# Order of operand stores and result loads on the SyncE queue at the turn from the up projection to the down projection

## The chip, the cores and the metric

The kernel runs on one core of a Trainium2 chip. The metric is the device time of one execution in microseconds (us); the time of a version is the median of its runs.

## What is computed

One step of a one-layer hybrid encoder over 640 tokens (512 of a prompt and 8 x 16 of samples), all in float32: an input projection, two groups of attention heads, an output projection, and a SwiGLU feed-forward network with a residual and a final norm. The change touches the feed-forward network only. Of the reference this is:

```
def merge_and_ffn(x, oa, ob, norm_grp_a, norm_grp_b, w_out, norm_ffn, w_gate, w_up, w_down):
    o = jnp.concatenate([rmsnorm(oa, norm_grp_a), rmsnorm(ob, norm_grp_b)], axis=-1)
    x = x + o @ w_out
    h = rmsnorm(x, norm_ffn)
    return x + (jax.nn.silu(h @ w_gate) * (h @ w_up)) @ w_down
```

The model width is 2048, the feed-forward width 5632 (44 tiles of 128, taken as 22 pairs, numbered 0 to 21).

## The kernel before

Tensors lie with features on the 128 partitions and tokens along the row; the 640 tokens are two halves of 320. Every float32 product is made from three reduced-precision matmuls: an operand is split into a high part (ScalarE writes it, rounded) and a low part (VectorE subtracts the high part from the source), and `mm3` (lines 204 to 206) multiplies high by high, high by low and low by high.

The feed-forward products use a seven-product scheme for 2 x 2 blocks (`quartet`, from line 880 on). One quartet takes four blocks of weights, forms three sums of them on VectorE and two on GpSimd (lines 932 and 941), splits each of seven weight operands (lines 195 and 196), and yields seven products, in the order p1, p6, p7, p2, p5, p4, p3. The right-hand operands are seven prepared combinations of the activations, called `which` 0 to 6, each with its two split halves in one tile of 128 x 640.

**Gate and up.** For each of the 22 pairs there is one quartet for `w_gate` and one for `w_up` with eight tiles a block, so 24 matmuls a product. After a pair's up quartet its seven combinations are formed. They must be kept for the down projection and SBUF can't hold those of 22 pairs, so `store_part` writes one of them to DRAM after each product that follows: split, as two transfers of 128 x 320 to `act_d` (ScalarE writes the high part into a scratch tile `half`, line 992, of which there are two; VectorE the low part, line 994; stores at lines 995 and 996), or, for the pairs in `raw_pairs`, unsplit, as one transfer to `first_d`.

**Down.** There are 32 steps. Step t adds to two tiles of the result, q = t % 8 and q + 8, the contributions of the pairs that `active(t)` lists: a pair stays active for eight steps in turn, so five or six pairs are in SBUF at a time. Pairs 0 to 4 are active in step 0; their last steps in this first round are 0, 2, 3, 5 and 6. A step is one quartet with five or six tiles a block, 7 x 5 x 3 = 105 matmuls for five. In the first eight steps the two result tiles (the residual `x2_d`) are loaded when the step is emitted (lines 1081 and 1082).

**The turn.** During the last up quartet, after each product, `free(which)` (lines 963 to 979) frees the gate/up operands of that `which` and brings in those of the five pairs of step 0: the pairs in `raw_pairs` (1, 2, 3) are loaded unsplit from `first_d` by SyncE, two pairs a load, and split there: the high part on ScalarE (line 973), the low part on VectorE for the first of a load and on GpSimd for the second (line 974). Pairs 0 and 4 are loaded split from `act_d` by a DMA that GpSimd issues (`fetch`, line 958). When a pair is given up in steps 0 to 7, its tiles go back to the free list, and if it is in `raw_pairs`, its split form is first written to `act_d`, for use in a later round (line 1074). The operands of the pair that comes next are fetched by GpSimd into tiles from the free list.

**What sets the order.** The program emits instructions in the order of the Python code. A scheduler then orders each engine's queue; within the data dependences it may issue a transfer ahead of others that were emitted before it. SyncE issues nearly all loads and stores, one after the other, and one that waits holds up those behind it; GpSimd's queue, too, is in order and holds its elementwise work and the operand fetches. Functions named `keep_...` add ordering edges: `keep_turns` lets a buffer's users stay in order, and `keep_behind` (lines 153 to 169) keeps the ScalarE instructions recorded in `n.behind` behind the last instruction on that engine emitted before them. Tiles come from 62 buffers `S` of 128 x 640 and 12 buffers `W` of 128 x 1024; a buffer that is put back is the last to be taken again.

Of the kernel before, what the change touches and what calls it, by code (L numbers as in the profile page):

```python
# [13 lines left out]
P = 128  # L14
# [3 lines left out]
HT = 320  # L18
# [31 lines left out]
class Net:  # L50
# [104 lines left out]
    def keep_behind(self):  # L155

        info = mybir.DependencyInfo(mybir.DependencyClass.NoSync, mybir.DependencyReason.DATA)
        for k, block in enumerate(self.nc.cur_f.blocks):
            inside = [0] * (len(block.instructions) + 1)
            for a, b in self.behind:  # L160
                if k < len(a):
                    inside[a[k]:b[k]] = [1] * (b[k] - a[k])
            last = None
            for i, ins in enumerate(block.instructions):
                if ins.engine == mybir.EngineType.Activation:
                    if not inside[i]:
                        last = ins
                    elif last is not None:
                        self.tc.add_manual_dep(ins, last.name, info, reason="behind")

    def keep_held(self):

# [127 lines left out]
def build(nc, tc, io, pools):  # L300
    n = Net(nc, tc, io, pools)
# [15 lines left out]
    def dram(name, shape):  # L317
        return pools["dr"].tile(list(shape), F32, tag=name, name=name)
# [491 lines left out]
    own_b, acts_b = group_operands(ob_d, g_b, ssq, range(8))  # L810
    n.add("decode", decode_a(1))
    x2_d, act_d = dram("x2_d", (KT, P, TOK)), dram("act_d", (7, P, NPAIR, 2, HT))
    first_d = dram("first_d", (7, P, 3, HT))
    r_a, ssq_a = n.get("S"), n.get("S")
    for m in range(KT):
        ps = n.dense([(io["w_out_b"][m], 8)], acts_b)
# [141 lines left out]
        nc.gpsimd.dma_start(out=r(sh(t, 2, HT)), in_=r(act_d[which, :, j]))  # L958
        lefts[j][which] = t, hl

    raw_pairs = active(0)[1:4]

    def free(which):
        n.put("S", *(h[which][0] for h in hs))
# [100 lines left out]
    def step(t, part="all"):  # L1065
# [4 lines left out]
        def after(which):  # L1070
            gone = [j for j in now if j not in nxt]
            for j in gone:
                if j in raw_pairs and t < 8:
                    dma(out=act_d[which, :, j], in_=sh(lefts[j][which][0], 2, HT))
            n.put("S", *(lefts[j][which][0] for j in gone))
            waiting.append([(j, which) for j in nxt if j not in now])
            fetch_waiting(2)

        if t < 8:
            x, y = n.get("S"), n.get("S")  # L1080
            dma(out=x, in_=x2_d[q])
            dma(out=y, in_=x2_d[q + 8])
            sums.append((x, y, n.get("S") if q % 2 == 0 else sums[-1][2]))
        x, y, u = sums[q]
        c11, c21, c12, c22 = x[:, :HT], x[:, HT:], y[:, :HT], y[:, HT:]
# [3 lines left out]
        for name, bank in quartet(cnt, load, [lefts[j] for j in now], None, after, part):  # L1089
# [20 lines left out]
                add(c21, c21, bank)  # L1110
            elif name == "p3":
                add(c12, c12, bank)
            store_part()
            yield name

    def run(*args):
# [51 lines left out]
    at = n.emitted()  # L1168
# [99 lines left out]
```

## Time and profile before

| | us |
|---|---|
| median of 3 runs | 2648.95 |
| lowest and highest run | 2647.41, 2651.69 |
| the profiled execution's own time | 2648.2 |
| span of its profile | 2646.4 |

The profile is of one execution. Of its span PE (the matmul engine, TensorE) is busy 98%, VectorE (DVE) 75%, ScalarE (ACT) 40% and GpSimd (POOL) 25%. The page divides the span into 40 slices of 66 us; in all but a few of them PE is at 9 tenths or more. The chain of waits is made of PE for 72%, of VectorE for 5% and of DMA for 4%. The granted TensorE clock over the span is 0.994 of full speed.

### The profile page before, as it was taken

What the parts mean: (1) busy time and instruction counts of PE and PEld (TensorE: products, weight loads), DVE (VectorE), ACT (ScalarE), POOL (GpSimd) and SP (SyncE); (2) the same over time, 40 slices, a digit from 0 to 9 for tenths busy, and PEclk for the clock granted to TensorE, in tenths of its full rate; (3) what the DMA queues carried; (4) which work ended last, traced back from release to release, by engine and by line L of the source; (5) the groups of instructions that cost most, each with busy time, mean ns of one, the idle gap of its engine ahead of it and who ended that gap; (6) DMA issues with size and microseconds to landing.
All of it is one profiled execution on the core that took longest, in us unless ns stands there. A gap on an engine that the chain in (4) does not pass through costs nothing.

```text
span 2646.4 us, 45166 instructions
## 1 busy us (share of the span) xinstructions
PE 2584.1 (98%) x17565; PEld 2527.2 (95%) x17565; DVE 1978.9 (75%) x3071; ACT 1069.3 (40%) x1732; POOL 662.1 (25%) x577
## 2 busy tenths in 40 slices
PE   8999999999999999999999999999999799999997
PEld 8999998999899999999999999999999799999996
DVE  5665566655866888768888888888887677777797
ACT  5443344444633553333443433433444333333343
POOL 0000000000201203333333233233234432333353
PEclk9999999999999999999999999999999899999998
DMA  5322232434655433333433433433436975665655
GB/s 170 105 70 83 87 101 92 129 116 133 216 186 183 156 127 123 115 106 123 142 130 125 140 130 125 144 132 120 150 128 214 372 201 155 170 184 169 185 155 178
DMA packets 178678, 388.47 MB, mean 147 GB/s; under 512 B 21856, under 2 KB 70496, under 8 KB 178464
## 3 DMA queue, kind: packets, MB, share of 16 engines
q1 hardware_dynamic: 153120, 329.21, 38.5%
q0 software_dynamic: 24192, 55.06, 7.3%
q8 instruction: 138, 2.26, 0.4%
q10 hardware_dynamic: 1152, 1.31, 0.1%
q14 instruction: 76, 0.62, 0.1%
HBM read 301.90 MB, written 82.87 MB: 145 GB/s over the span
## 4 chain that ended last, share of the span: by engine, by line
PE 72%; DVE 5%; DMA 4%; ACT 1%; issue 1%; POOL 0%; SPq 0%; DVEq 0%; ACTq 0%
PE dn L204 15%; PE dn L206 15%; PE dn L205 14%; PE at L204 9%; PE at L206 9%; PE at L205 9%; DVE W L196 2%; DMA W<-w_down 1%; PE at L321 1%; DVE S L951 1%; DMA act_d<-half 1%; DMA S<-cka 0%; DMA S<-first_d 0%; ACT W L195 0%; PE at L402 0%
## 5 line engine op out<-in xcount | busy, mean ns | idle before, releaser
L204 PE MATMUL dn<-S,W 128*128 128x320 f32 x3694 | 1158.3, 314 | 5.0 <-ACT W L195 4.4
L206 PE MATMUL dn<-S,W 128*128 128x320 f32 x3694 | 1145.1, 310 | 12.2 <-DVE W L196 12.2
L205 PE MATMUL dn<-S,W 128*128 128x320 f32 x3694 | 1143.8, 310 | 1.1 <-DVE S L200 0.8
L195 ACT ACTIVATE W<-W 128x1024 fp32r<-128x1024 f32 (+2 forms) x632 | 608.2, 963 | 977.5 <-PE dn L205 542.5
L196 DVE TENSOR_TENSOR W<-W,W 128x1024 fp32r<-128x1024 f32 (+2 forms) x632 | 738.4, 1169 | 91.8 <-ACT W L195 88.3
L204 PEld LDWEIGHTS dn<-S,W 128*128 128x128 f32 x3694 | 695.0, 188 | 17.5 <-ACT W L195 6.1
L206 PEld LDWEIGHTS dn<-S,W 128*128 128x128 f32 x3694 | 694.4, 188 | 17.1 <-DVE W L196 15.9
L205 PEld LDWEIGHTS dn<-S,W 128*128 128x128 f32 x3694 | 694.8, 188 | 3.6 <-DVE S L200 1.0
L204 PE MATMUL at<-S,W 128*128 128x320 f32 x1594 | 494.5, 310 | 7.5 <-ACT W L195 7.5
L206 PE MATMUL at<-S,W 128*128 128x320 f32 x1594 | 495.0, 311 | 4.3 <-DVE W L196 4.3
L205 PE MATMUL at<-S,W 128*128 128x320 f32 x1594 | 493.9, 310 | 0.0
L932 POOL TENSOR_TENSOR W<-W,W 128x1024 f32<-128x1024 f32 (+2 forms) x75 | 159.4, 2126 | 641.9 <-DVE W L196 404.8
L204 PEld LDWEIGHTS at<-S,W 128*128 128x128 f32 x1594 | 300.6, 189 | 8.3 <-ACT W L195 8.3
L206 PEld LDWEIGHTS at<-S,W 128*128 128x128 f32 x1594 | 300.4, 188 | 6.5 <-DVE W L196 6.5
L205 PEld LDWEIGHTS at<-S,W 128*128 128x128 f32 x1594 | 300.5, 189 | 0.0
L951 DVE TENSOR_TENSOR S<-S,dn 128x320 f32<-128x320 f32 x358 | 163.7, 480 | 71.1 <-PE dn L206 71.0
L941 POOL TENSOR_TENSOR W<-W,W 128x1024 f32<-128x1024 f32 (+2 forms) x75 | 162.9, 2173 | 115.0 <-DVE W L196 105.1
L927 DVE TENSOR_TENSOR W<-W,W 128x1024 f32<-128x1024 f32 (+2 forms) x76 | 122.4, 1610 | 70.1 <-DMA W<-w_down 36.5
L951 DVE TENSOR_TENSOR S<-S,at 128x320 f32<-128x320 f32 x262 | 123.2, 480 | 51.4 <-PE at L206 50.5
L958 POOL DMA_DIRECT2D S<-act_d x168 | 91.7, 547 | 185.6 <-PE dn L206 94.5
L929 DVE TENSOR_TENSOR W<-W,W 128x1024 f32<-128x1024 f32 (+2 forms) x76 | 83.4, 1097 | 63.0 <-DMA W<-w_up 34.2
L994 DVE TENSOR_TENSOR S<-S,half 128x320 fp32r<-128x320 f32 x133 | 115.1, 886 | 13.5 <-ACT half L992 11.6
(153 smaller groups left out, 2125.8 us busy)
## 6 DMA issues: line engine op xcount, KB each, us to landing
S<-act_d POOLq DMA_DIRECT2D x168, 320.0 KB, 3.9
W<-w_gate SPq DMA_DIRECT2D x88, 512.0 KB
W<-w_up SPq DMA_DIRECT2D x88, 512.0 KB
W<-w_in SPq DMA_DIRECT2D x66, 512.0 KB
W<-w_down SPq DMA_DIRECT2D x64, 384.0 KB
W<-w_down SPq DMA_DIRECT2D x68, 320.0 KB
act_d<-half SPq DMA_DIRECT2D x133, 160.0 KB
act_d<-S SPq DMA_DIRECT2D x133, 160.0 KB
```

The lines of the kernel that those rows point to most:

```text
L195: self.nc.scalar.activation(hi, src, AF.Identity)
L196: self.nc.vector.tensor_tensor(lo, src, f(hi), ALU.subtract)
L204: mm(out, a[0], b[0], start=first, stop=False)
L205: mm(out, a[0], b[1], start=False, stop=False)
L206: mm(out, a[1], b[0], start=False, stop=last)
L927: nc.vector.tensor_tensor(b12[:, w], b12[:, w], b22[:, w], sub)
L929: nc.vector.tensor_tensor(s6[:, w], b11[:, w], b12[:, w], sub)
L932: eng.tensor_tensor(b11[:, w], b22[:, w], s6[:, w], sub)
L941: eng.tensor_tensor(b21[:, w], b21[:, w], s6[:, w], sub)
L951: add = lambda o, a, b: nc.vector.tensor_tensor(o, a, b, ALU.add)
L958: nc.gpsimd.dma_start(out=r(sh(t, 2, HT)), in_=r(act_d[which, :, j]))
L994: nc.vector.tensor_tensor(r(src), src, hi, ALU.subtract)
```

## The change

Three edits, on the functions `keep_behind`, `free`, `step` and the table `raw_pairs`:

1. `keep_behind` is extended from ScalarE to SyncE, and the SyncE transfers of two places are recorded in `n.behind`: the stores of given-up operand tiles (line 1074 before, 1076 after) and the loads of the two result tiles (1081 and 1082 before, 1085 and 1086 after). On SyncE each of them is issued behind the last transfer not so recorded that was emitted before it.
2. `raw_pairs` grows from the pairs 1, 2, 3 to 1, 2, 3, 4. Pair 4 is written unsplit to `first_d` in the gate/up part, split at the turn, and its split form is stored to `act_d` when it is given up at the end of step 6.
3. The seven combinations of the last pair (21) are stored from step 2 on, not from step 0 on. (One part is stored directly behind the last up quartet, as before.)

```
@@ keep_behind
-            last = None
-            for i, ins in enumerate(block.instructions):
-                if ins.engine == mybir.EngineType.Activation:
-                    if not inside[i]:
-                        last = ins
-                    elif last is not None:
-                        self.tc.add_manual_dep(ins, last.name, info, reason="behind")
+            for engine in (mybir.EngineType.Activation, mybir.EngineType.SP):
+                last = None
+                for i, ins in enumerate(block.instructions):
+                    if ins.engine == engine:
+                        if not inside[i]:
+                            last = ins
+                        elif last is not None:
+                            self.tc.add_manual_dep(ins, last.name, info, reason="behind")
@@ build
-    first_d = dram("first_d", (7, P, 3, HT))
+    first_d = dram("first_d", (7, P, 4, HT))
-    raw_pairs = active(0)[1:4]
+    raw_pairs = active(0)[1:]
@@ step
                 if j in raw_pairs and t < 8:
+                    at = n.emitted()
                     dma(out=act_d[which, :, j], in_=sh(lefts[j][which][0], 2, HT))
+                    n.behind.append((at, n.emitted()))
...
             x, y = n.get("S"), n.get("S")
+            at = n.emitted()
             dma(out=x, in_=x2_d[q])
             dma(out=y, in_=x2_d[q + 8])
+            n.behind.append((at, n.emitted()))
...
-            store_part()
+            if t > 1:
+                store_part()
             yield name
```

How the queues stand before and after, at three places. In the rows, an operand `S_3183_21528` is a tile in an S buffer (the numbers only tell tiles apart), `W_...` a weight tile, `half_...` a scratch tile; a row reads out<-in.

**SyncE at the turn, from the first weight load of step 0 on.** Before:

```order
L914 DMA W_3254_21847<-w_down 128x640
L996 DMA act_d<-S_3125_21061 128x320
L1074 DMA act_d<-S_3183_21528 128x640
L968 DMA S_3185_21534<-first_d 128x320
L968 DMA S_3194_21581<-first_d 128x320
L1074 DMA act_d<-S_3184_21531 128x640
L968 DMA S_3191_21573<-first_d 128x640
L914 DMA W_3255_21849<-w_down 128x640
L1074 DMA act_d<-S_3186_21536 128x640
L968 DMA S_3202_21621<-first_d 128x640
```

After the change:

```order
L915 DMA W_3247_21826<-w_down 128x640
L997 DMA act_d<-S_3118_21033 128x320
L969 DMA S_3178_21506<-first_d 128x640
L969 DMA S_3187_21554<-first_d 128x640
L969 DMA S_3184_21546<-first_d 128x640
L915 DMA W_3248_21828<-w_down 128x640
L969 DMA S_3195_21595<-first_d 128x640
L969 DMA S_3198_21603<-first_d 128x640
L969 DMA S_3206_21645<-first_d 128x640
L915 DMA W_3249_21830<-w_down 128x640
```

The stores from line 1074 have gone from between the unsplit loads, and the loads that were 128 x 320 are 128 x 640.

**SyncE where the last pair's parts (lines 995 and 996) and the given-up tiles are stored.** Before, with the weight loads of step 1 (line 914) between them:

```order
L914 DMA W_3292_22054<-w_down 128x640
L995 DMA act_d<-half_21877 128x320
L1074 DMA act_d<-S_3233_21767 128x640
L996 DMA act_d<-S_3173_21486 128x320
L996 DMA act_d<-S_3152_21296 128x320
L995 DMA act_d<-half_21903 128x320
L996 DMA act_d<-S_3152_21296 128x320
L995 DMA act_d<-half_21932 128x320
L996 DMA act_d<-S_3141_21226 128x320
L914 DMA W_3293_22056<-w_down 128x640
```

After the change the first weight load below is the second of step 2, and the last is the third of step 3:

```order
L915 DMA W_3308_22173<-w_down 128x640
L915 DMA W_3309_22175<-w_down 128x640
L1076 DMA act_d<-S_3176_21500 128x640
L915 DMA W_3322_22264<-w_down 128x640
L1076 DMA act_d<-S_3207_21647 128x640
L915 DMA W_3344_22383<-w_down 128x640
L915 DMA W_3345_22385<-w_down 128x640
L996 DMA act_d<-half_22202 128x320
L996 DMA act_d<-half_22229 128x320
L915 DMA W_3346_22387<-w_down 128x640
```

The first store of a given-up tile now stands behind eleven of the weight loads of steps 0 to 2, and the parts that were moved (six of the last pair's seven, two stores each) behind all twelve.

**GpSimd in steps 2 and 3: the weight sums (932 and 941 before, 933 and 942 after) and the operand fetches (958, 959).** Before, from the first sum of step 2:

```order
L932 TENSOR_TENSOR W_3322_22226<-W_3321_22224,W_3323_22229 128x640
L941 TENSOR_TENSOR W_3332_22300<-W_3332_22300,W_3323_22229 128x640
L958 DMA S_3424_22834<-act_d 128x640
L958 DMA S_3429_22861<-act_d 128x640
L958 DMA S_3432_22885<-act_d 128x640
L958 DMA S_3436_22910<-act_d 128x640
L932 TENSOR_TENSOR W_3353_22408<-W_3352_22406,W_3354_22411 128x640
```

After the change, from the second sum of step 2:

```order
L942 TENSOR_TENSOR W_3322_22264<-W_3322_22264,W_3310_22178 128x640
L959 DMA S_3384_22598<-act_d 128x640
L959 DMA S_3387_22622<-act_d 128x640
L959 DMA S_3417_22813<-act_d 128x640
L959 DMA S_3422_22840<-act_d 128x640
L933 TENSOR_TENSOR W_3346_22387<-W_3345_22385,W_3347_22390 128x640
L959 DMA S_3425_22864<-act_d 128x640
L959 DMA S_3429_22889<-act_d 128x640
L959 DMA S_3432_22912<-act_d 128x640
L942 TENSOR_TENSOR W_3358_22465<-W_3358_22465,W_3347_22390 128x640
```

Four fetches stand ahead of step 3's first weight sum in both; after the change three more stand ahead of its second. All seven write into buffers whose earlier content SyncE stores during steps 2 and 3: given-up tiles of the pairs 1 and 2, and parts of the last pair.

## Rows read from the trace of the kernel before

**Rows 1.** The page: tenths of PE and GB/s of DMA, 40 slices.

```profile
PE   8999999999999999999999999999999799999997
...
GB/s 170 105 70 83 87 101 92 129 116 133 216 186 183 156 127 123 115 106 123 142 130 125 140 130 125 144 132 120 150 128 214 372 201 155 170 184 169 185 155 178
```

**Rows 2.** Windows: us, busy PE, PEld, DVE, ACT, POOL (x instructions), clock, DMA share, GB/s.

```profile
1160.00:1220.00 60.00, 60.00 (x411) 60.00 (x410) 45.83 (x50) 22.51 (x27) 19.26 (x10) 1.00 0.37 117
...
1980.00:2030.00 50.00, 50.00 (x342) 49.76 (x341) 40.69 (x47) 19.58 (x29) 17.27 (x11) 1.00 0.45 141
...
2030.00:2120.00 90.00, 71.43 (x423) 66.91 (x423) 59.59 (x91) 30.81 (x54) 42.67 (x54) 0.91 1.08 369
2120.00:2180.00 60.00, 60.00 (x411) 60.00 (x410) 45.66 (x72) 21.40 (x32) 20.82 (x25) 1.00 0.68 195
...
2030.00:2060.00 30.00, 21.66 (x126) 19.65 (x125) 20.06 (x29) 12.99 (x26) 21.06 (x26) 0.94 1.09 374
2060.00:2090.00 30.00, 21.54 (x109) 19.54 (x110) 18.36 (x29) 7.95 (x15) 13.47 (x20) 0.77 1.13 389
2090.00:2120.00 30.00, 28.24 (x191) 27.71 (x190) 21.17 (x35) 9.87 (x15) 8.14 (x10) 1.00 1.02 343
...
2021.50:2115.50 94.00, 75.43 (x449) 70.67 (x448) 63.76 (x91) 34.52 (x60) 47.53 (x56) 0.91 1.02 347
```

**Rows 3.** Waits, 2030 to 2120: us in total, times, longest.

```profile
ACT half L992 <- DMA act_d<-half: 16.3, 4, 7.3
...
POOL W L932 <- DMA act_d<-S: 8.7, 1, 8.7
```

**Rows 4.** Chain of waits, 1980 to 2200: start us, us, what.

```profile
2028.00 4.51 DMA S<-first_d
...
2034.98 3.39 POOL W L941
2038.38 3.39 DMA W<-w_down
...
2048.43 7.02 DMA S<-first_d
...
2059.71 7.96 DMA S<-x_d
2067.74 11.63 DMA act_d<-half
...
2105.58 6.77 DMA W<-w_down
```

**Rows 5.** SyncE's timeline: first store at the turn; step 4's first weight load (second of two).

```profile
2021.87 0.32 SPq L1074 DMA_DIRECT2D act_d<-S  x1
...
2115.49 2.56 SPq L914 DMA_DIRECT2D W<-w_down  x2
```

**Rows 6.** Tile act_d, 2030 to 2120: GpSimd's fetches (ns min/median/max, from, to); transfers' time to landing.

```profile
L958 POOL DMA_DIRECT2D S<-act_d x38: 527/547/591, 2029.6 to 2116.9; - x38
...
DMA to landing us min/median/max: 4.5/7.0/11.8
```

**Rows 7.** Line 974, 2020 to 2060: ns min/median/max.

```profile
L974 DVE TENSOR_TENSOR S<-S,S x14: 477/493/1860, 2021.3 to 2056.0; 128x320 fp32r<-128x320 f32 x14
...
L974 POOL TENSOR_TENSOR S<-S,S x7: 862/1094/1556, 2025.6 to 2053.6; 128x320 fp32r<-128x320 f32 x7
```

**Rows 8.** GpSimd's timeline: first and last of 15 fetches during step 0.

```profile
2060.17 2.69 POOL L958 DMA_DIRECT2D S<-act_d  x5
...
2080.49 1.59 POOL L958 DMA_DIRECT2D S<-act_d  x3 [1.59 <-DVE S L994]
```

**Rows 9.** PE's timeline: the first matmul of step 3.

```profile
2120.39 0.31 PE L204 MATMUL dn<-S,W 128*128 128x320 f32 x1
```

**Rows 10.** Timelines of GpSimd and VectorE: start us, us, instruction.

```profile
2027.78 1.83 POOL L1040 TENSOR_TENSOR S<-S,S 128x640 f32<-128x640 f32 x1
...
2028.09 1.86 DVE L974 TENSOR_TENSOR S<-S,S 128x320 fp32r<-128x320 f32 x1
```

## The prediction

> **What bounds the kernel now.** I read the page's slices first, then a table of windows, then the waits and the chain of the one stretch that stood out. In the slices [rows 1] PE is at 9 tenths or more in all but three of 40; away from the kernel's two ends only one is lower, slice 32, and it is also the slice with the most DMA traffic, 372 GB/s. The windows [rows 2] place it: from 2030 to 2120 us PE ran 423 matmuls, while in the 60 us behind it ran 411 and was never idle. At that rate, 6.85 a microsecond or 0.146 us each, 90 us hold 616.5, so 193.5 are missing: **28.2 us were lost** here, part as idle time, part at a mean granted clock of 0.91. The 50 us ahead of it and the 60 behind it have PE busy throughout. By thirds the loss is 11.6 us (126 matmuls of 205.5), 14.1 us (109) and 2.1 us (191), which is 27.8; edges make the difference. This is the turn: the last up quartet and the steps 0 to 2. The DMA engines moved 369 GB/s over it and 389 in its middle third, against 195 behind it; I take 389 as what they can carry here.
>
> What PE waited for is behind two chains [rows 4]. First, unsplit operands (4.51 us from issue to landing, then 7.02), with GpSimd's weight sum (3.39) and a weight load (3.39) between. Second, the stores of the last pair's high parts: a result load and then one such store landed 7.96 and 11.63 us after issue. ScalarE stood 16.3 us in four waits for its two scratch tiles [rows 3], and the weight splits for PE are behind it in its queue. Both are one cause: too much traffic in the same 90 us, with stores that nobody needs soon issued among loads that PE needs next.
>
> **The change, part by part.**
>
> *Stores of given-up tiles go back in the queue.* Counted on SyncE's order from the first of these stores (issued at 2021.87 [rows 5]): ahead of step 1's first weight load stand 6,240 KB before and 5,120 after; ahead of step 4's, 20,640 and 18,880. Before, 5 such stores of 320 KB precede step 1's first load and all 21 step 4's; after, none and 14. What gets ahead of them is what PE needs next; what has to wait for them is GpSimd's fetches into the same buffers (a rival below).
>
> *Pair 4 raw.* In the gate/up part 7 high parts on ScalarE, 7 low parts on VectorE and 7 of 14 stores go. PE is busy 60.00 us of 60 in a stretch there [rows 2], so I cost this at nothing; its cover is PE itself. At the turn 7 fetches of 320 KB go from GpSimd (2,240 KB, and 7 x 0.547 = 3.8 us of its queue [rows 6]), and 7 x 160 KB of unsplit loads come (already in the counts above), with 7 high parts on ScalarE, which stays under half busy [rows 2], and 7 low parts on GpSimd, 7 x 1.094 = 7.7 us [rows 7]. GpSimd was busy 21 us of the 30 from 2030, so 3.9 us more fit, but one more subtraction stands ahead of the last up quartet's weight sum, on the first chain: 1.1 us. The 7 later stores, 2,240 KB at the end of step 6, come where the traffic was 195 GB/s: 5.9 us of DMA time at 389, no PE time.
>
> *Last pair's parts from step 2.* 12 stores of 160 KB (128 x 320 values) leave step 0; ScalarE's four waits for scratch tiles leave with them. Four buffers of 62 are held two steps longer; fetches run more than a pair ahead, so nothing to at most 4 x 0.84 us (320 KB at 389) is lost. I take nothing.
>
> *Result loads behind.* Those of step 0 come behind the unsplit loads. The nearest row is the 7.96 us of one at the turn, the upper end if an addition waits for it; the lower end is a gain, since it no longer delays an operand. I take nothing, since fewer bytes stand ahead.
>
> **The sum.** First third: to step 1's first load 1,120 KB on SyncE and 2,240 KB of fetches fewer, 3.44 MB, 8.8 us at 389; of 11.6 us 2.8 remain, with GpSimd's 1.1 that is **3.9**. Second third: the parts are now stored in step 2. There SyncE's order holds 4,800 KB and GpSimd's 7 fetches, 7,040 KB or 7.2 MB in a step's 15.3 us (105 matmuls of 0.146); 389 carry 6.0, so 1.2 MB or 3.2 us too much. Before, the same stores in step 0 stood among 4,320 KB and 15 fetches [rows 8], 9.3 MB, 8.7 us too much. So 3.2/8.7 of 14.1 remains: **5.2**. Last third: **2.1** as it is. Kept 11.2, given back 28.2 - 11.2 = **17.0**. The profiled execution took 2648.2, so 2631.2. The median shown is 2648.95, 0.03% above; I predict **2631**.
>
> As a check on the whole, the DMA's account to step 4's first load: before 20,640 KB and some 39 fetches (38 from 2029.6 on [rows 6], one just ahead), 33.9 MB in the 93.6 us to 2115.49 [rows 5]; after 18,880 KB and 32 fetches, 29.8 MB. From 2021.9 that lasts to 2098.6 at 389, to 2107.8 at the mean of the stretch, 347 [rows 2]. Step 3 begins at 2120.39 [rows 9]; without the loss step 4 would at 2120.39 - 28.2 + 15.3 = 2107.5, and its first load has to be issued at least a landing of 6.77 us [rows 4] earlier, at 2100.7. So the queue alone costs from nothing to 7.1 us, less than the 11.2 I keep. With full recovery the time is 2620.0.
>
> "DMA: Bandwidth & Descriptors" in the Trainium skill (section "Where 436 GB/s comes from") puts a limit of about 358 GB/s on a core's HBM traffic; while this case's row has 389 over 30 us, so the trace decides. By 358 the same sum would keep 3.1 + 6.4 + 2.1 = 11.6 us: 2631.6.
>
> **The rivals.**
>
> *The queue stays the bound, only shorter.* For it: 14 stores are still ahead of step 4's loads. Against it: they stand where PE has weights in hand. PE then gains only what leaves the queue: 33.9 - 29.8 = 4.1 MB, 10.5 us: 2637.7.
>
> *The scratch chain moves whole.* If stores land as late in step 2 as the 11.63 us of before, all 14.1 us come back instead of 5.2: 2640.1.
>
> *VectorE is held up by the added subtractions.* On line 974 VectorE's subtraction took 0.493 us in the median and 1.86 at most [rows 7]; the longest began at 2028.09, inside a GpSimd operation of 1.83 us from 2027.78 [rows 10]. Seven more GpSimd subtractions at up to 1.86 - 0.493 = 1.37 us are 9.6 us on the chain that splits weights: 2640.8. "SBUF — State Buffer" of the Trainium skill (section "Who interferes with whom") says that a VectorE instruction with two SBUF inputs contends with a GpSimd instruction that reads SBUF. By that rule the trace agrees, with those two rows; but most of VectorE's are near the median.
>
> *No change.* All transfers to step 8's first weight load grow by 3,360 KB on SyncE less 2,240 of fetches: 1.1 MB, 2.9 us. If the DMA engines are full up to there, stores put off are only paid later: 2651. Against it: the 60 us behind the turn run at 195 GB/s.
>
> *Slower: GpSimd's queue waits for the late stores.* Three fetches now stand ahead of step 3's second weight sum, into buffers whose store is only just issued. The first sum feeds the fifth product, the second the sixth, 8.8 and 11 us into the step (2.2 a product); from the point where a store lands later than that, PE waits. Before, such a wait was 8.7 us long [rows 3] and hidden. Were it uncovered in the five steps 3 to 7, 43.5 us against 28.2 given back: 2663.5.
>
> **How the numbers follow.** My forecast 0.56; the queue as bound 0.13; scratch chain 0.10; VectorE 0.05; no change 0.09; GpSimd slower 0.07. A measurement of this kernel tells about 0.2%, 5.3 us, from no change. Faster by more than that: 0.56 + 0.13 + 0.10 + 0.05 = 0.84; within: 0.09; slower: 0.07. The range goes from full recovery less a microsecond of edges, 2619, over the three weaker gains to the edge of no change, 2644, and leaves out 0.16.
>
> **What would show it.** Right: the turn's 90 us hold over 530 matmuls; ScalarE's wait for scratch tiles is gone from step 0 and is below 6 us in step 2; unsplit loads land in under 4.5 us; GB/s behind the turn rises from 195 to about 300. Wrong: PE idle in steps 2 to 4 behind ScalarE's splits; GpSimd idle behind stores ahead of its weight sums, with PE idle after; VectorE's line 974 above 1 us in the mean; or the dip unchanged in length.

## The result and the profile after

| | before | after |
|---|---|---|
| median of 8 runs each, us | 2650.43 | 2657.11 |
| lowest and highest run, us | 2647.41, 2652.31 | 2651.80, 2658.61 |
| the profiled execution's own time, us | 2648.2 | 2657.07 |

The ratio is 1.0025, with an interval of 1.0014 to 1.0035: the change made the kernel **slower by 6.7 us**, where 2631 and a gain of some 18 were forecast.

The slices of the page after the change, beside [rows 1]: slice 32 has lost its 7, but 31 and 32 are now both 8, and the traffic that stood in one slice (372 GB/s) stands in two.

```profile
PE   8999999999999999999999999999998899999997
...
GB/s 172 105 74 78 91 100 89 131 120 128 219 183 189 150 127 124 120 98 106 152 118 132 147 115 135 145 123 129 142 128 215 276 294 152 176 184 157 195 155 177
```

The windows after the change, same columns as [rows 2]: the turn, its thirds, and what follows.

```profile
2030.00:2120.00 90.00, 76.00 (x460) 74.74 (x458) 69.57 (x93) 33.30 (x61) 45.31 (x52) 0.89 0.85 275
2030.00:2060.00 30.00, 20.55 (x117) 19.79 (x116) 29.93 (x29) 14.37 (x31) 24.36 (x26) 0.84 0.91 295
2060.00:2090.00 30.00, 26.76 (x151) 26.53 (x150) 19.12 (x31) 7.35 (x13) 13.22 (x18) 0.82 0.87 280
2090.00:2120.00 30.00, 28.69 (x196) 28.42 (x194) 20.52 (x34) 11.57 (x20) 7.73 (x9) 1.00 0.78 251
2120.00:2150.00 30.00, 24.54 (x133) 22.55 (x134) 17.03 (x27) 7.49 (x11) 8.05 (x9) 0.89 0.81 287
2180.00:2210.00 30.00, 27.39 (x176) 27.13 (x176) 22.76 (x36) 9.63 (x13) 7.20 (x8) 0.94 0.52 144
2150.00:2200.00 50.00, 46.94 (x306) 46.08 (x305) 34.67 (x54) 15.92 (x24) 15.84 (x18) 0.97 0.83 275
```

With the prediction's 6.85 matmuls a microsecond, each window's loss is its length less its matmuls at that rate. Below, "loss" is always this, from one profile; the columns are windows of 30 us by their start, and the last sums the ten windows from 1970 to 2270:

| us lost | 2030 | 2060 | 2090 | 2120 | 2150 | 2180 | 1970 to 2270 |
|---|---|---|---|---|---|---|---|
| before | 11.6 | 14.1 | 2.1 | -0.1 | -0.2 | -0.1 | 26.9 |
| after | 12.9 | 8.0 | 1.4 | 10.6 | 0.8 | 4.3 | 37.2 |

So the turn's 90 us gave back 5.5 us (27.8 to 22.3), by the second third, and two **new dips**, at 2120 and 2180, where PE had been busy throughout, took 15.7 (with the 0.8 between them). The difference, 10.3, answers to the 8.9 us between the two profiled executions.

**Where the first new dip comes from.** First the DMA engines' traffic in 40 slices of 1 us from 2080, after the change:

```profile
GB/s 371 169 33 32 223 90 0 51 148 394 72 87 376 233 261 15 0 0 0 115 213 315 13 150 348 384 399 376 310 142 294 369 392 397 374 397 332 352 397 405
```

The same slices before:

```profile
GB/s 407 412 396 399 375 379 384 384 396 417 411 375 238 389 407 407 402 412 407 230 230 379 151 189 325 356 387 405 394 341 413 300 297 392 405 379 280 358 272 348
```

For 24 us the DMA engines now moved little, and then they ran full. Windows of 24 and 46 us after the change put sizes on it:

```profile
2080.00:2104.00 24.00, 24.00 (x165) 24.00 (x164) 17.81 (x28) 8.78 (x14) 4.75 (x3) 1.00 0.50 140
2104.00:2150.00 46.00, 39.23 (x234) 36.97 (x233) 26.58 (x45) 13.60 (x22) 12.62 (x15) 0.93 0.89 311
```

And before:

```profile
2080.00:2104.00 24.00, 21.52 (x127) 20.27 (x126) 17.93 (x28) 8.92 (x14) 7.75 (x8) 0.88 1.06 357
2104.00:2150.00 46.00, 44.55 (x304) 44.28 (x303) 34.16 (x55) 15.86 (x24) 13.84 (x15) 1.00 0.76 237
```

From 357 to 140 GB/s in 24 us are 5.2 MB that did not move while there was room; 3.4 MB of them moved in the next 46 us, on top of what moves there anyway. SyncE's timeline after the change shows what was issued meanwhile. L915 is the weight load, L996 and L997 store the last pair's parts, L1076 given-up tiles, L1085 and L1086 load result tiles; the second number is how long the group lasted, waits within it included.

```profile
2074.38 12.61 SPq L915 DMA_DIRECT2D W<-w_down  x3
2087.04 0.42 SPq L1076 DMA_DIRECT2D act_d<-S  x1
2090.01 0.33 SPq L915 DMA_DIRECT2D W<-w_down  x1
2090.39 0.43 SPq L1076 DMA_DIRECT2D act_d<-S  x1
2092.23 6.29 SPq L915 DMA_DIRECT2D W<-w_down  x2
2100.22 0.80 SPq L996 DMA_DIRECT2D act_d<-half  x2
...
2114.79 0.45 SPq L1085 DMA_DIRECT2D S<-x_d  x1
2115.28 0.91 SPq L1086 DMA_DIRECT2D S<-x_d  x1
2116.23 1.88 SPq L1076 DMA_DIRECT2D act_d<-S  x2
2118.16 0.49 SPq L915 DMA_DIRECT2D W<-w_down  x1
2118.69 3.26 SPq L1076 DMA_DIRECT2D act_d<-S  x4
...
2123.86 6.53 SPq L915 DMA_DIRECT2D W<-w_down  x4
```

From 2074 to 2099 SyncE issued six weight loads, two stores and nothing else: a weight load waits for a free weight buffer, and the given-up tiles that have been put behind it wait too, though the kernel before could store the first of them from 2021.87 on [rows 5] and the DMA engines move nothing for whole microseconds. SyncE's waits from 2060 to 2130 (us in total, times, longest), after the change:

```profile
SPq L915 <- DVE W L197: 26.3, 7, 8.1
```

and before, where SyncE had stores to issue in between:

```profile
SPq L914 <- DVE W L196: 15.1, 7, 5.0
```

The order on the queue does not make this gap alone. In two runs described below, e1 (edit 1 alone) and e13 (edits 1 and 2), 335 and 337 GB/s moved in the same 24 us; in e3 (edit 3 alone) 345; in e6, which has edit 3 and no store of a given-up tile at all, 150. So the stretch is empty where the parts' stores have left it (edit 3) and the stores of given-up tiles are not there to fill it.

Then, from 2100 to 2122, twelve stores of parts, twelve of given-up tiles and the two result loads of step 3 went out almost together, with step 3's last two weight loads among them (2118.16 is the last), and step 4's four only from 2123.86, where its first was one of the two issued at 2115.49 before [rows 5]. The timelines of VectorE, PE and ScalarE show what it did (in brackets the idle time just before the instruction, and what ended it):

```profile
2120.75 0.88 DVE L952 TENSOR_TENSOR S<-S,dn 128x320 f32<-128x320 f32 x2 [6.83 <-DMA S<-x_d]
2121.39 0.39 PE L205 MATMUL dn<-S,W 128*128 128x320 f32 x1 [2.70 <-DVE S L952]
...
2123.66 0.47 PE L205 MATMUL dn<-S,W 128*128 128x320 f32 x1
...
2125.16 0.74 ACT L196 ACTIVATE W<-W 128x640 fp32r<-128x640 f32 x1 [8.00 <-DMA W<-w_down]
...
2136.80 0.41 PE L205 MATMUL at<-S,W 128*128 128x320 f32 x1 [2.33 <-ACT W L196]
```

An addition waited 6.83 us for a result tile whose load had been put back (issued at 2114.79), PE stood behind it, then ran its matmuls at the lower clock (0.47 us where 0.31 is usual; 0.72 of the full clock granted in the mean from 2120 to 2125, so part of that stretch stood at the lower of the two levels, 1.2 GHz), and step 3's last weights, issued behind the same stores, ended a wait of 8.00 us on ScalarE. The second dip looks like the end of the same account, which no run tested by itself: from 2150 to 2200 the traffic is 275 GB/s after and 179 before, 4.8 MB more, and PE did 306 matmuls where it had done 343, 5.4 us. Before:

```profile
2150.00:2200.00 50.00, 50.00 (x343) 50.00 (x342) 37.08 (x57) 17.59 (x25) 16.93 (x20) 1.00 0.63 179
```

**The first third** kept its whole loss although its traffic fell from 374 [rows 2] to 295 GB/s. Here VectorE was never idle, 29.93 of 30 us. Its subtraction of the turn, beside GpSimd's (line 975, 2020 to 2060, ns min/median/max; [rows 7] before):

```profile
L975 DVE TENSOR_TENSOR S<-S,S x14: 476/1141/4447, 2019.7 to 2056.5; 128x320 fp32r<-128x320 f32 x14
...
L975 POOL TENSOR_TENSOR S<-S,S x14: 868/1116/1857, 2024.0 to 2055.1; 128x320 fp32r<-128x320 f32 x14
```

Its median went from 0.493 to 1.141 us with 14 subtractions on GpSimd instead of 7. "SBUF — State Buffer" in the Trainium skill (section "Who interferes with whom") says that a VectorE instruction with two SBUF inputs contends with a GpSimd instruction that reads SBUF; these rows agree.

### The profile page after: what moved, and what is told of

Its sections match the earlier page's. It is cut to its first block, busy times and chain, and to the rows that moved or that the text cites. A ratio compares the mean times of both kernels' runs of the same rounds, so it can differ in the third digit from the quotient of the medians.

```text
span 2655.3 us, 45136 instructions
## 1 busy us (share of the span) xinstructions
PE 2591.2 (98%) x17565; PEld 2535.0 (95%) x17565; DVE 1981.5 (75%) x3064; ACT 1069.2 (40%) x1732; POOL 666.0 (25%) x577
## 5 line engine op out<-in xcount | busy, mean ns | idle before, releaser
L205 PE MATMUL dn<-S,W 128*128 128x320 f32 x3694 | 1161.9, 315 | 11.3 <-ACT W L196 4.8
L205 PEld LDWEIGHTS dn<-S,W 128*128 128x128 f32 x3694 | 698.0, 189 | 23.4 <-issue 10.6
L933 POOL TENSOR_TENSOR W<-W,W 128x1024 f32<-128x1024 f32 (+2 forms) x75 | 159.1, 2122 | 644.0 <-DVE W L197 446.5
L928 DVE TENSOR_TENSOR W<-W,W 128x1024 f32<-128x1024 f32 (+2 forms) x76 | 127.7, 1680 | 75.9 <-DMA W<-w_down 41.8
L930 DVE TENSOR_TENSOR W<-W,W 128x1024 f32<-128x1024 f32 (+2 forms) x76 | 84.1, 1107 | 69.1 <-DMA W<-w_up 34.2
L995 DVE TENSOR_TENSOR S<-S,half 128x320 fp32r<-128x320 f32 x126 | 109.0, 886 | 2.1 <-ACT half L993 0.4
```

The costliest lines, as they stand in the source:

```text
L205: mm(out, a[0], b[0], start=first, stop=False)
L928: nc.vector.tensor_tensor(b12[:, w], b12[:, w], b22[:, w], sub)
L930: nc.vector.tensor_tensor(s6[:, w], b11[:, w], b12[:, w], sub)
L933: eng.tensor_tensor(b11[:, w], b22[:, w], s6[:, w], sub)
L995: nc.vector.tensor_tensor(r(src), src, hi, ALU.subtract)
```

## The experiments

Three theories stood at the start: that VectorE, held up by GpSimd's added subtractions (edit 2), is what costs (theory A); that the put-off stores of edit 1, which come back as a burst, do (theory B); that the late parts of edit 3 only carry their chain to step 2 (theory C). None had edit 3 costing anything. Differences are of medians (11 runs each; 5 for e11 and e15 to e18) against the kernel before, timed beside each.

| run | what it is | us | to before | ratio (interval) | loss |
|---|---|---|---|---|---|
| e1 | edit 1 alone | 2648.73 | -1.5 | 0.9996 (0.9987, 1.0004) | 27.0 |
| e2 | edit 2 alone | 2651.65 | +1.4 | 1.0004 (0.9995, 1.0012) | 27.4 |
| e3 | edit 3 alone | 2655.26 | +5.0 | 1.0022 (1.0014, 1.0031) | 33.3 |
| e4 | after, fewer subtractions on GpSimd | 2655.07 | +4.9 | 1.0017 (1.0008, 1.0026) | 34.6 |
| e5 | before, split form stored early | 2647.77 | -1.4 | 0.9996 (0.9987, 1.0005) | 24.5 |
| e6 | e5 and edit 3 | 2646.51 | -2.7 | 0.9991 (0.9982, 1.0000) | 24.1 |
| e7 | before, four buffers held | 2653.65 | +4.5 | 1.0017 (1.0008, 1.0026) | 30.2 |
| e8 | edit 3, but from step 5 | 2653.76 | +4.6 | 1.0015 (1.0007, 1.0024) | 33.1 |
| e9 | before, fetches held back | 2649.63 | -2.0 | 0.9988 (0.9979, 0.9997) | 25.5 |
| e10 | after, fetches held back | 2656.48 | +4.8 | 1.0015 (1.0006, 1.0024) | 33.4 |
| e11 | e5 and e9 | 2644.28 | -7.4 | 0.9968 (0.9955, 0.9980) | 22.0 |
| e12 | e9, fetches emitted sooner | 2648.41 | -3.3 | 0.9987 (0.9978, 0.9996) | 24.7 |
| e13 | after without edit 3 | 2653.23 | +2.1 | 1.0010 (1.0001, 1.0019) | 31.4 |
| e14 | e13, four buffers held | 2655.90 | +4.8 | 1.0017 (1.0008, 1.0026) | 33.4 |
| e15 | e11 and edit 3 | 2642.04 | -9.1 | 0.9966 (0.9953, 0.9978) | 18.8 |
| e16 | e11 and edit 2, as in e4 | 2642.47 | -8.7 | 0.9966 (0.9954, 0.9979) | 18.8 |
| e17 | e11, edit 3 and edit 2 as in e4 | 2640.36 | -10.3 | 0.9961 (0.9948, 0.9973) | 16.8 |
| e18 | e17, result loads behind | 2641.86 | -8.8 | 0.9965 (0.9952, 0.9979) | 18.7 |

### Each edit alone, and fewer subtractions on GpSimd (e1 to e4)

e1, e2 and e3 have the diff's edits 1, 2 and 3, one each, on the kernel before. e4 is the changed kernel with

```
-                (nc.vector, nc.gpsimd)[a].tensor_tensor(lo, part, f(hi), ALU.subtract)
+                (nc.vector, nc.gpsimd if j == raw_pairs[0] else nc.vector)[a].tensor_tensor(lo, part, f(hi), ALU.subtract)
```

> Edit 1 alone (stores and result loads behind; three pairs raw; last pair stored from step 0). Theory A, that the fourth raw pair's seven GpSimd subtractions block VectorE at the turn (VectorE busy 10.0 of 10 us in the three windows from 2030 after the change): without them this is faster than before by 5 to 10 us. Theory B, that the put-off stores come back as one burst ahead of step 4's weight loads (2123.86 instead of 2115.49): slower than before by 3 to 10 us, with PE short of 60 or more matmuls between 2110 and 2150 again.

> Edit 2 alone (pair 4 raw, nothing moved behind). Theory A: slower than before by 5 to 10 us, line 974 on VectorE at 1.2 us in the mean as after the change (0.74 before). Theory B: no slower than before, perhaps faster by 2 to 5 us, since 1,120 KB less pass at the turn.

> Edit 3 alone (last pair's parts from step 2, stores of given-up tiles early as before). Theories A and B both: faster than before by 5 to 12 us, since ScalarE's 16.3 us of waits for scratch tiles leave step 0 and nothing is added. Theory C, that the parts only carry their chain to step 2: within 3 us of before.

> The changed kernel, with the low parts of the pairs 3 and 4 both on VectorE (seven subtractions moved from GpSimd to VectorE). Theory A: the loss from 2030 to 2060 falls from 12.3 to under 6 us and the time from 2657 to about 2650. Theory B: the turn may gain 2 to 4 us, the dip between 2110 and 2150 stays at 10 us or more, the time within 4 us of the changed kernel.

Edits 1 and 2 alone can't be told from nothing; edit 3 alone costs 5.0 us. So e1 came out as neither A nor B had it, e2 against A, and e3 against all three: A and B had it faster by 5 to 12 us, C within 3. e4 is near what B had. In e3 the new losses lie at 2090 (6.9 us) and 2120 (6.1), while the second third loses less than before (9.9 for 14.1). VectorE's and PE's timelines of e3:

```profile
2095.24 0.83 DVE L927 TENSOR_TENSOR W<-W,W 128x640 f32<-128x640 f32 x1 [7.99 <-DMA S<-x_d]
...
2097.26 0.63 PE L206 MATMUL dn<-S,W 128*128 128x320 f32 x1 [4.97 <-DVE W L196]
```

VectorE's weight sum starts after 7.99 idle us, which the profile puts down to a result load that landed then, and PE waits 4.97 us for the split that follows it. Theory A is real as a mechanism and small as a price: in e4 the subtraction on VectorE is back at 0.48 us,

```profile
L975 DVE TENSOR_TENSOR S<-S,S x21: 476/480/3944, 2023.5 to 2055.3; 128x320 fp32r<-128x320 f32 x21
```

the first third's loss goes from 12.9 to 9.4, and e4 is some 2 us below the changed kernel (4.9 against 6.7 above before, of two comparisons that are each uncertain by about as much). In e2 the median is as high, 1.148 us, and the whole costs nothing measurable.

### What in edit 3 costs (e5 to e8)

e5 takes the stores of given-up tiles away altogether: the split form of the pairs 1 to 3 is stored in the gate/up part, where the unsplit form is, and stays valid.

```
@@ store_part
-            if j in raw_pairs:
-                dma(out=first_d[which, :, j - raw_pairs[0]], in_=src)
-            else:
...
+            at = n.emitted()
+            hi = n.scratch()
...
@@ after the seven combinations of pair i
+                if i in raw_pairs:
+                    for j, which, src, _ in parts:
+                        dma(out=first_d[which, :, j - raw_pairs[0]], in_=src)
@@ step
-                if j in raw_pairs and t < 8:
-                    dma(out=act_d[which, :, j], in_=sh(lefts[j][which][0], 2, HT))
```

e6 adds edit 3 to it. e7 leaves the parts where they are in the kernel before and only returns their four buffers at the end of step 2; e8 is edit 3 with another bound.

```
@@ e7: store_part, step
-            n.put("S", *done)
+            if j == NPAIR - 1:
+                kept.extend(done)
+            else:
+                n.put("S", *done)
...
             store_part()
+            if t == 2 and name == "p3":
+                n.put("S", *kept)
@@ e8: step
+            if t > 4:
+                store_part()
```

> The kernel before, with the split form of the pairs 1 to 3 stored to act_d in the gate/up part (beside the unsplit one), so that no given-up tile is stored in the steps: 21 stores of 320 KB less at the turn, 42 of 160 KB more where DMA runs at 117 GB/s. Theory D (the loss at the turn is set by how many bytes pass there): 6.9 MB less, 10 to 18 us faster than before. Theory L (the loss is made of single late transfers, and bytes taken away elsewhere only move it): within 4 us of before.

> The same with edit 3 (last pair's parts from step 2). Theory B (edit 3 costs its 5 us because the parts' 12 stores meet the stores of given-up tiles ahead of the weight loads of the steps 3 and 4): with those gone edit 3 costs nothing, this is as fast as the kernel with early stores or up to 5 us faster. Theory H (edit 3 costs because four buffers are held until step 2, so result loads and fetches come later): 5 us slower than the kernel with early stores alone.

> The kernel before, with the last pair's four buffers given back only at the end of step 2; its parts are stored in step 0 as before. Theory H: 3 to 6 us slower than before. Theory B: within 2 us of before.

> Edit 3 alone, with the parts stored from step 5 on instead of step 2. Theory B: the parts leave the crowded steps, 3 us or more faster than with step 2 (2655.3), so 2652 or less. Theory H: buffers are held longer, 2655 or more.

e5 came out as theory L had it. Of B and H each had one run right, e6 for B and e7 for H; e8, at 2653.76, fell between the two.

Holding four buffers, with no store moved, costs 4.5 us, near the 5.0 of edit 3; storing the parts still later, which holds edit 3's buffers longer, is no worse (e8). But e7 does not copy what edit 3 holds. The first of the last pair's parts is stored directly behind the last up quartet with edit 3 as well, and its buffer goes back there; so edit 3 holds three buffers, which come back one by one during step 2, and e7 holds four to that step's end. The loss also lies elsewhere: in e7 the second third loses 16.6 us and the last 5.0, and the window from 2120 nothing, where e3 has 9.9, 6.9 and 6.1. The chain of waits of e7 is that of [rows 4], about as long in its first two links (before: 7.96 and 11.63) and longer in a third:

```profile
2062.46 8.06 DMA S<-x_d
...
2070.59 11.70 DMA act_d<-half
...
2082.87 6.26 DMA act_d<-half
```

This third link before:

```profile
2079.95 4.54 DMA act_d<-half
```

Where no given-up tile has to be stored, the same edit 3 costs nothing (e6 is 1.3 us below e5). So its price needs those stores beside it. Whether that is because buffers come late while others must first be stored, or because the parts' stores and theirs meet on the way, these runs don't tell apart.

e6 is not free of the late dip, though. It gains in the second third (6.6 us lost, 13.8 in e5) and loses 5.0 us from 2120, where e5 loses nothing. The window of e6, and two weight loads of its chain of waits, issued among and behind the parts' stores:

```profile
2120.00:2150.00 30.00, 27.32 (x171) 27.33 (x172) 21.66 (x35) 8.78 (x14) 7.08 (x8) 0.89 0.46 132
```

```profile
2104.97 7.41 DMA W<-w_down
...
2112.75 7.82 DMA W<-w_down
```

e5 tells something about the bytes. 21 stores of 320 KB leave the first steps, 6.9 MB or 17.7 us of DMA time at 389 GB/s, and 1.4 us of time come back. But before, only seven of them were issued in the two thirds that lose (2.3 MB, 5.9 us at 389), and twelve from 2090 to 2120, where PE loses little. In those two thirds 1.6 us of loss come back. The windows of e5:

```profile
2030.00:2060.00 30.00, 22.72 (x135) 21.03 (x133) 21.85 (x27) 11.83 (x24) 20.43 (x26) 0.92 1.06 347
2060.00:2090.00 30.00, 22.07 (x111) 20.66 (x112) 20.29 (x32) 9.41 (x18) 14.73 (x20) 0.80 1.07 360
2090.00:2120.00 30.00, 28.58 (x195) 28.31 (x195) 21.89 (x36) 9.91 (x16) 9.45 (x10) 1.00 0.67 200
```

The traffic falls by a few per cent in the first two thirds and by two fifths in the last. GpSimd's fetches don't move up into the room: 17, 16 and 6 are issued in the three thirds, as before.

### Fetches held back (e9 to e12)

GpSimd's operand fetches of the steps 0 to 7 are kept behind the work emitted ahead of them, as ScalarE's copies are:

```
@@ keep_behind
+            for engine in (mybir.EngineType.Activation, mybir.EngineType.Pool):
@@ fetch_waiting
+                at = n.emitted()
                 fetch(j, which)
+                if held:
+                    n.behind.append((at, n.emitted()))
@@ after, in step
-            fetch_waiting(2)
+            fetch_waiting(2, t < 8)
```

e9 is that on the kernel before, e10 on the changed kernel (with SyncE in the list of engines as well), e11 on e5; e12 is e9 with `fetch_waiting(0, t < 8)`.

> The kernel before, with the operand fetches that are emitted in the steps 0 to 7 kept on GpSimd's queue behind the last instruction emitted before them, so that they no longer run two to four steps ahead into every free buffer. Theory F (the fetches ahead fill the DMA engines at the turn, and whatever else is taken away there is filled up by them): GB/s from 2060 to 2090 falls from 389 to under 330, the turn's loss of 28 us to 18 or less, the time to 2640 or less. Theory L (the loss is a chain of single waits at the turn that has nothing to do with depth): within 4 us of before, or slower by what later fetches cost.

> The changed kernel with the same hold on the fetches. Theory F: the put-off stores no longer meet the fetches, the dips between 2110 and 2190 shrink from 15 us to under 6, the time to 2645 or less. Theory L: as the changed kernel, 2654 to 2660.

> Early stores (no given-up tile stored in the steps) with the hold on the fetches. Theory F: the fastest of all, 5 us or more below the hold alone, since now 6.9 MB less do leave the turn. Theory L: within 4 us of before.

> The kernel before with the hold on the fetches, each emitted two products sooner (one pair ahead, but with 13 instead of 9 us before its operand is needed). Theory F, if the hold alone makes PE wait for operands in the steps 1, 3, 4: 3 us or more faster than the hold alone. If the fetches are in time there: the same within 2 us.

On the kernel before, theory F failed in all of its figures: 339 GB/s from 2060 to 2090, 24.9 us of loss at the turn, 2649.63 us. e10 is as theory L had it, e11 as F had it. e12 is 1.2 us below e9, so fetches that come too late are not what limits e9.

Held fetches are worth 2.0 us on the kernel before, and with them the removal of the 21 stores is worth 5.4 (e11 against e9), where it was 1.4 without. One reason can be seen: with held fetches GpSimd issues 6 from 2060 to 2090 instead of 16, and SyncE issues 8 stores of given-up tiles there instead of 3, so stores take part of the room. That the two together give more than their sum is not clear of the noise, since each of these differences is uncertain by 2 to 3 us. The first two thirds of e11, against 374 and 389 GB/s before [rows 2]:

```profile
2030.00:2060.00 30.00, 23.90 (x141) 22.36 (x140) 22.02 (x26) 13.27 (x26) 19.53 (x24) 0.92 0.99 320
2060.00:2090.00 30.00, 24.28 (x123) 23.16 (x122) 22.51 (x36) 9.80 (x18) 11.20 (x13) 0.74 0.91 294
```

Even here 22.0 us of loss remain, at 294 to 320 GB/s. In e10 held fetches cure little: the windows from 2120 to 2210 lose 13.0 us where they lost 15.7, and the time, 2656.48 us, can't be told from the changed kernel's. So its dips don't come, in the main, from fetches that run ahead.

### Edit 3 out, buffers held without it (e13, e14)

e13 is the changed kernel with this edit, e14 the same with e7's.

```
-            if t > 1:
-                store_part()
+            store_part()
```

> The changed kernel with edit 3 undone: the last pair's parts are stored from step 0 on, as before; stores and loads behind, and pair 4 raw, as in the change. Theory H (the held buffers and late parts of edit 3 cost it all): the time is that of before, 2649 to 2653 us, and the dips at 2110 to 2150 and at 2180 are gone. Rival P (the put-off stores of edit 1, 14 of them between steps 3 and 8, make the late dips by themselves): 2654 us or more, and the windows 2120 to 2150 still lose over 5 us.

> The kernel of the run above with one more edit: the buffers of the last pair's parts are stored from step 0 on, but are returned to the free list only at the end of step 2. If holding buffers is what costs in the changed kernel, as it did by itself (2653.65 against 2649.17 us): 4 to 6 us over the run above, with losses behind 2110. If it is the meeting of the parts' stores with the put-off stores: within 2 us of the run above.

Neither side of e13's expectation came out clean: 2.1 us remain without edit 3 (interval 0.3 to 5), and the window from 2120 still loses 4.6 us where the changed kernel lost 10.6. There, too, VectorE waits for a weight load that stands behind put-off stores. The window and the wait in e13:

```profile
2120.00:2150.00 30.00, 27.11 (x174) 26.84 (x174) 18.85 (x31) 8.79 (x13) 6.90 (x7) 0.94 0.75 249
```

```profile
2129.07 0.83 DVE L928 TENSOR_TENSOR W<-W,W 128x640 f32<-128x640 f32 x1 [5.89 <-DMA W<-w_down]
```

So the window from 2120 loses 0.9 us with edit 1 alone (e1), 2.7 with edit 2 alone (e2), 4.6 with both (e13), 6.1 with edit 3 alone (e3), 5.0 with edit 3 and no store of a given-up tile (e6), and 10.6 with all three edits. Edit 3 makes such a dip without any put-off store, and edits 1 and 2 together make one without edit 3; in the changed kernel the two about add up. These are single profiles.

Holding four buffers as well, in e14, takes the time's difference from 2.1 to 4.8 (with runs that overlap), a rise of 2.7 where 4 to 6 us were expected; its new loss lies at 2090 (7.4 us), not at 2120, and its profile is of the longest of its runs (2661.14 us). What is left to the changed kernel's 6.7, 1.9 us, can't be told from nothing, so whether the late parts cost beside their buffers stays open.

### Towards a faster kernel (e15 to e18)

With the stores gone and the fetches held, the change's edits were added again: edit 3 (e15), edit 2 with e4's line (e16), both (e17), and both with the part of edit 1 that puts the result loads behind (e18).

```
@@ e18: keep_behind, step
-            for engine in (mybir.EngineType.Activation, mybir.EngineType.Pool):
+            for engine in (mybir.EngineType.Activation, mybir.EngineType.SP, mybir.EngineType.Pool):
...
+            at = n.emitted()
             dma(out=x, in_=x2_d[q])
             dma(out=y, in_=x2_d[q + 8])
+            n.behind.append((at, n.emitted()))
```

> The fastest kernel so far (split form of the pairs 1 to 3 stored early, the fetches of the steps 0 to 7 held behind on GpSimd; 2644.28 us) with edit 3 added. If edit 3's only harm is buffers that come late while stores are put off, there is little harm here and its gain in scratch waits shows: 2641 to 2645. If held buffers cost by themselves: 2648 to 2650.

> The fastest kernel so far with edit 2 added (pair 4 raw, low parts of the pairs 3 and 4 on VectorE, its split form stored early too). Seven operand fetches of 320 KB leave the turn's start and seven unsplit 160 KB come. If bytes at the turn count once the fetches ahead are held: 2639 to 2643. If the unsplit load chain (load, split, subtraction) is what PE waits for: 2644 to 2648.

> Early split stores, fetches held, pair 4 raw and the last pair's parts from step 2. Each of the last two gave about 2 us on top of the fastest kernel, with losses left of 18.8 us each where it had 22.0. If the two gains lie in different windows and add: 2639 to 2641 and a loss under 17 us. If both remove the same wait: 2642 to 2645, as either alone.

> The kernel of the run above with the part of edit 1 that orders the loads of the result tiles behind on SyncE. If the order on SyncE's queue matters once the queue is short: 1 to 3 us below the run above. If not: within 1 us of it. If additions now wait for result tiles: over 2 us above it.

**e17 is the fastest kernel**, 2640.36 us, 10.3 below before. Edit 3, which cost 5.0 us by itself, is no loss on top of e11 and by the medians a gain of 1.7 (e15); edit 2, as in e4, of 1.3 (e16). Each of these steps is smaller than the intervals are wide, and their sum from e11 to e17 (2.9 us, of two comparisons) too; that e17 is faster than before is beyond doubt, that it is faster than e11 is not. By its figures e17 is the case in which the two gains add (2639 to 2641 us, a loss under 17), but these intervals don't decide it. Ordering the result loads behind gives nothing (1.5 us above e17, with overlapping runs). e17's windows:

```profile
2030.00:2060.00 30.00, 23.19 (x136) 22.44 (x135) 28.38 (x38) 15.19 (x32) 16.89 (x19) 0.89 0.97 330
2060.00:2090.00 30.00, 29.97 (x205) 29.67 (x204) 26.42 (x41) 10.35 (x16) 11.55 (x12) 1.00 0.66 200
2090.00:2120.00 30.00, 26.92 (x165) 26.27 (x165) 20.13 (x33) 10.84 (x19) 10.51 (x14) 0.89 0.96 303
```

The second third, which lost 14.1 us before, loses 0.1. The first still loses 10.1, as in every version (7.1 to 12.9 us), and what remains moves to the last.

## Why the prediction was wrong

**The bottleneck was named rightly, and its price wrongly.** The place was right: 27.8 us are lost at the turn, and between the kernel's two ends its slices show no other such place. The step that failed first is the sum's rule that bytes taken out of the queue are PE time given back at 389 GB/s ("of 11.6 us 2.8 remain"). In the first third the traffic did fall, from 374 to 295 GB/s, and PE got nothing for it: 12.9 us lost where 3.9 were forecast. Edit 2's added subtractions hide a part of it (e4 loses 9.4 there), but e5, which has none of them, shows the same: by the rule the 2.3 MB of stores that left the two thirds that lose are 5.9 us, and 1.6 came back. Nor did the single edits bring the 17.0 us: edit 1 alone is 1.5 us faster and edit 2 alone 1.4 slower, neither clear of noise (e1, e2), and both together are 2.1 us slower (e13). The chains of [rows 4] suggest that PE waits here for single transfers and splits, each behind its own load, and not for the volume; no run tests that by itself.

**Nothing was set down for the time behind the turn**, and this turned the sign: the turn gave back 5.5 us, and the windows from 2120 to 2210 took 15.7. Three terms of the sum say so. The stores that edit 1 puts back stand in it as a gain only, with what they cost later left to the rivals; with edit 2 they go with a loss of 4.6 us from 2120 (e13). The parts moved to step 2 were priced inside the turn only; e3 loses 6.1 us from 2120 and is 5.0 us slower. And "Four buffers of 62 are held two steps longer ... I take nothing": by the program edit 3 holds three, and a hold of four cost 4.5 us (e7; the interval holds 2 to 7), with the bound of 4 x 0.84 = 3.4 us inside that interval. So edit 3 was the costly one; how much of its 5.0 us is the hold and how much the late stores stays open.

**"Result loads behind ... I take nothing, since fewer bytes stand ahead"**: an addition did wait for one, 6.83 us, and PE 2.70 of it. The 7.96 of the upper end was the right size. The assumption behind it, and behind the check on the whole queue, was that the DMA engines run at 347 to 389 GB/s until step 4's first load. They ran at 275 over the turn, with the gap from 2080 to 2104 that edits 1 and 3 leave together. Step 4's first load was due at 2100.7 if the loss was gone; it came at 2123.86.

**The second third** (8.9 of 14.1 to be given back) was nearest: 6.1 came back. ScalarE's wait for scratch tiles left step 0 as the text said it would, and in step 2 it was 2.3 us, under the 6 named. Pair 4's 1.1 us for a further subtraction on GpSimd was too small for the first third, where e4 recovers 3.5 us of loss, but the time shows only about 2 of it.

**The rivals.** Slower, at a chance of 0.07, was the case that came, but not by its mechanism: GpSimd's fetches did wait for stores (11.3 us in four waits in the turn), yet PE's idle time behind 2118 ends with an addition and with weight splits, not with GpSimd's sums. Nearest in mechanism was the case of no change, "stores put off are only paid later": against it stood that the 60 us behind the turn ran at 195 GB/s, so there seemed to be room. There was; but the stores came into it in bursts and ahead of loads. No rival had the put-off transfers miss free time at the turn's end. VectorE's rival was right in mechanism (the subtraction's mean is 1.2 us, above the 1 us that the text named for it) and too dear: 9.6 us against about 2 in e4, which is itself no clear difference.

Of the signs named, the turn's matmuls came out wrong (460, not over 530), VectorE's line 974 (now 975) stood as the text had it for wrong, and so did PE's idle time behind ScalarE's splits (2.33 us at 2136.80); the GB/s behind the turn rose as for right, to 287 in the window from 2120, where it went with a loss.

**What stays open.** Why the first third loses 7 to 13 us in all versions: VectorE is full in the changed kernel, in e13 and in e14, but not before (20.06 of 30 us, [rows 2]), where the loss is much the same. And what in edit 3 costs: that it does cost is shown by e3, and that it doesn't where no given-up tile is stored by e6. Whether its buffers or its late stores do it was not separated, because e7 holds more than edit 3 does and loses its time elsewhere. A run with edit 3's own three buffers held, or one with the late parts in other buffers, would tell.

## What to carry to other kernels

A transfer put at the back of an in-order queue waits not only for the DMA engines but for what the queue's head waits for; before putting stores back, look at how long the head (here weight loads without a free buffer) stands still, whether the DMA engines are idle meanwhile, and what else comes when the held stores do. By itself the putting back cost nothing here (e1); with edits 2 and 3 it met other late stores. Don't turn bytes into PE time at the DMA rate: look first at how many of them pass in the stretch that loses (seven of 21 stores here), and test a removal alone and together with others (1.4 and 5.4 us here, a difference that the noise allows). Don't take a buffer held longer for free because the transfer that it delays is short; and when testing such a term, hold just the buffers that the change holds.

## What was not expected of the hardware

VectorE's 128x320 subtraction took 1.14 us in the median and up to 4.4 beside twice as many subtractions on GpSimd, against 0.49 before; a 128x640 weight sum took 3.87 us, where 0.83 is usual:

```profile
2031.16 3.87 DVE L928 TENSOR_TENSOR W<-W,W 128x640 f32<-128x640 f32 x1
```

That VectorE was busy for nearly the whole first third (29.93 of 30 us after the change, 29.97 in e2) was hardly visible in the time: e2 is 1.4 us above before, which can't be told from nothing.
